# Transposes of attention probabilities in single PSUM banks instead of a pair of banks

## The chip, the cores and the metric

The kernel runs on one core of one Trainium2 chip. The metric is the time of one execution in device microseconds (us), smaller is better; the figure for the kernel before is the median of 3 runs.

## What is computed

One step of a small hybrid diffusion backbone with two trunk layers, all in float32, over 512 latent tokens and 128 context tokens with 1024 channels. Each layer projects the normed input, runs four token mixers on it, merges them through gates, and then runs a squared-ReLU MLP. Three mixers are attention: windowed grouped-query attention (8 heads), neighbourhood attention (4 heads) and multi-head latent attention (MLA, 4 heads). Cut to the part that matters here:

```python
def context_and_latent_layer(x, c, cache, lw):
    h = modulate(rms_norm(x, lw['g_attn']), sh1, sc1)
    cb, cc, cv, gq, gk, gv, nq, nk, nv, mq, mkv, mkr, gates = in_project(h, lw['w_in'])
    ...
    p = softmax_sink(jnp.concatenate([s_loc, s_ctx], axis=-1), sink)
    o = jnp.einsum('nbkgqs,nbskd->nbqkgd', p_loc, vb) + jnp.einsum('nbkgqs,nskd->nbqkgd', p_ctx, v_ctx)
    ...
    x = x + gt1 * merge_branches(gates, y_conv, y_gqa, y_na, y_mla, lw)
    x = x + gt2 * squared_relu_mlp(modulate(rms_norm(x, lw['g_mlp']), sh2, sc2), lw['w_ff1'], lw['w_ff2'])
```

## The kernel before

Every large product is made of three matmuls on float32 operands that are split in a high and a low part (`hi*hi`, `hi*lo`, `lo*hi`); the copy to `hi` is ScalarE's, the subtraction that gives `lo` VectorE's. A layer has an attention stage (`mixers`), a merge of the branches and an MLP. In the attention stage the input projections for later heads are the filler: `attend` runs the heads' blocks of 128 queries one after the other and calls `fill` between their steps, which issues some projection matmuls (L199 to L201, eight steps of three per half of the tokens).

A head has five blocks: four of latent queries and one of context queries (`ctx`). A block goes through `block_scores` (matmuls L479/L480, or L482 to L484 for MLA, then on VectorE the row minimum, L515 with a mask or L518 without), `block_exp` (ScalarE, L524), `block_norm` (the reciprocal L528 on VectorE, the product L529 on GpSimd), `block_T` (one TensorE transpose for each 128 keys, L538, then ScalarE's copy to the high part, L542), `block_lo` (VectorE's low part, L545), and, for each pair of blocks, `pair_pv` (L555, then ScalarE's copy L559) and `pair_out` (VectorE's additions into `y`, L568 to L578). The scores run three blocks ahead of the transposes: round i issues the transposes of block i, filler, the scores of block i+3, and filler.

PSUM has eight banks of 512 float32 per partition. In the attention stage they are dealt as `psum(4, 2)`: four single banks (`bank()`, tiles named `pr`: projections, `pair_pv`, MLA's products) and two pairs of banks (`banks2()`, tiles named `S2`, shown as `S` in the profile). Before the change a pair of banks serves the scores of a block, the transposes of a block and three transposes of values per layer (L414). A new tile takes a place whose earlier holder has been read for the last time; which place was chosen by the scheduler when the program was built, and TensorE waits at the new tile's first matmul until that last reader is done. TensorE's instructions stand in the order of the code. In the attention stage the order on VectorE, ScalarE, GpSimd and SyncE is the scheduler's.

A latent block has 4 or 5 pieces of 128 keys (6 in MLA), a context block has 1. Over both layers there are 160 blocks.

Of the kernel before, what the change touches and what calls it, by code (L numbers as in the profile page):

```python
# [12 lines left out]
ALU = mybir.AluOpType  # L13
# [4 lines left out]
P = 128  # L18
# [43 lines left out]
def _r(ap):  # L62
    return ap.bitcast(F32)


class Net:
# [464 lines left out]
    def block_T(self, B):  # L531
        nc = self.nc
        if B["u"] == 0:
            B["pair"]["pt"] = self.at.tile([P, 2, 6, 256], F32R, name="pt", tag="pt", bufs=2)
        pt, p, nb = B["pair"]["pt"], B["p"], B["nb"]
        tp = self.banks2()
        for i, s in enumerate(B["pos"]):
            nc.tensor.transpose(tp[:, s * P:(s + 1) * P], p[:, i * P:(i + 1) * P], self.ident)  # L538
        src = tp[:, :nb * P].rearrange("p (c q) -> p c q", q=P)
        qs = slice(B["u"] * P, (B["u"] + 1) * P)  # L540
        B["hi"], B["lo"], B["src"] = pt[:, 0, 0:nb, qs], pt[:, 1, 0:nb, qs], src
        nc.scalar.copy(B["hi"], src)  # L542

    def block_lo(self, B):
        self.nc.vector.tensor_tensor(B["lo"], B["src"], _r(B["hi"]), ALU.subtract)  # L545

    def pair_pv(self, R):

# [984 lines left out]
```

## Time and profile before

| | |
|---|---|
| median of 3 runs | 2441.95 us (2441.12 to 2443.48) |
| profiled execution, its own time | 2444.15 us |
| its span in the trace | 2442.4 us |
| TensorE busy | 2329.5 us (95%) |
| VectorE busy | 1400.2 us (57%) |
| ScalarE busy | 936.0 us (38%) |
| attention stages | about 70 to 421 us and 1265 to 1616 us of the span |

The span runs from the first to the last instruction that the profiler recorded; the execution's own time is 1.75 us longer. Busy time of TensorE is that of its matmuls, whose ends are modelled; weight loads have a row of their own (PEld). An idle time that is put down to another engine ("waited for") ends with that engine's instruction.

### The profile page before, as it was taken

Reading aid. Unit: us, or ns where it says so; the run is one execution under the profiler, and the core shown is the slowest. Engines: PE = TensorE matmul, PEld = TensorE weight load, DVE = VectorE, ACT = ScalarE, POOL = GpSimd, SP = SyncE. Lnnn points to the kernel's source line nnn. Section 1 sums busy time; section 2 is a strip of 40 time slices with the busy share of each in tenths; the row PEclk is TensorE's granted clock in tenths of the full one; section 3 lists DMA queues with packets and bytes.
Section 4 is the critical chain, followed back from the end, with each engine's and each line's share of the span. In section 5 each row is a group of like instructions: output and inputs, shape, how many; then the busy total and the mean of one; then the engine's idle time right before and its main releaser. Section 6 shows DMA issues by size and latency. Waiting matters only on the chain. (4 is left out here: it accounts for less than half of the span.)

```text
span 2442.4 us, 39683 instructions
## 1 busy us (share of the span) xinstructions
PE 2329.5 (95%) x15766; PEld 2265.1 (93%) x15766; DVE 1400.2 (57%) x2744; ACT 936.0 (38%) x1877; POOL 360.6 (15%) x468
## 2 busy tenths in 40 slices
PE   8889988999999999999998898899999999999998
PEld 4888878999999999999988897889999999999998
DVE  5776676566655777776467666753333454443433
ACT  5555554322224432322255555542222353231311
POOL 0323322111112000000123223211111110000001
PEclk9999989999999999999999999999999999999999
DMA  6322310544432344443231231033222212222222
GB/s 231 90 72 82 93 34 25 201 156 153 141 115 78 115 153 156 156 144 133 96 123 46 83 102 56 19 104 122 70 78 80 98 44 78 75 73 78 70 83 73
DMA packets 85322, 242.96 MB, mean 99 GB/s; under 512 B 9745, under 2 KB 31249, under 8 KB 83729
## 3 DMA queue, kind: packets, MB, share of 16 engines
q1 hardware_dynamic: 85136, 240.43, 29.3%
q8 instruction: 124, 2.03, 0.3%
q14 instruction: 62, 0.50, 0.1%
HBM read 222.14 MB, written 12.75 MB: 96 GB/s over the span
## 5 line engine op out<-in xcount | busy, mean ns | idle before, releaser
L199 PE MATMUL pr<-hhi,whiw 128*128 128x320 f32 (+1 forms) x2752 | 869.7, 316 | 2.7 <-ACT st L300 1.5
L201 PE MATMUL pr<-hhi,wlow 128*128 128x320 f32 (+1 forms) x2752 | 855.5, 311 | 2.3 <-DVE wlow L166 1.4
L200 PE MATMUL pr<-hlo,whiw 128*128 128x320 f32 (+1 forms) x2752 | 856.1, 311 | 0.0
L199 PEld LDWEIGHTS pr<-hhi,whiw 128*128 128x128 f32 (+1 forms) x2752 | 518.9, 189 | 4.6 <-ACT st L300 1.7
L201 PEld LDWEIGHTS pr<-hhi,wlow 128*128 128x128 f32 (+1 forms) x2752 | 518.3, 188 | 4.9 <-DVE wlow L166 2.6
L200 PEld LDWEIGHTS pr<-hlo,whiw 128*128 128x128 f32 (+1 forms) x2752 | 519.0, 189 | 3.4 <-DVE hlo L1159 2.5
L165 ACT CAST whiw<-raww 128x1024 fp32r<-128x1024 f32 x184 | 192.8, 1048 | 285.8 <-PE pr L200 266.7
L166 DVE TENSOR_TENSOR wlow<-raww,whiw 128x1024 fp32r<-128x1024 f32 x184 | 237.5, 1291 | 60.8 <-ACT whiw L165 60.2
L199 PE MATMUL pr<-hh,whiw 128*128 128x320 f32 x832 | 257.1, 309 | 0.0
L200 PE MATMUL pr<-hl,whiw 128*128 128x320 f32 x832 | 256.9, 309 | 0.0
L201 PE MATMUL pr<-hh,wlow 128*128 128x320 f32 x832 | 256.9, 309 | 0.0
L916 DVE SCALAR_TENSOR_TENSOR x<-pr,mod,x 128x256 f32<-128x256 f32 x320 | 107.7, 379 | 198.9 <-PE pr L201 196.8
L253 DVE SCALAR_TENSOR_TENSOR junk<-wm,cb 128x1024 bf16<-128x1024 f32 x160 | 195.6, 1222 | 40.9 <-DMA wm<-in_wm 37.8
L1114 POOL TENSOR_TENSOR sqs<-sqs,sq 128x320 f32<-128x320 f32 x48 | 47.6, 992 | 969.6 <-ACT sq L1112 941.9
L529 POOL TENSOR_SCALAR p<-p,sm 128x512 f32<-128x512 f32 (+3 forms) x160 | 118.6, 741 | 420.0 <-DVE sm L528 372.4
L524 ACT ACTIVATE p<-S,sm 128x641 f32<-128x641 f32 (+6 forms) x160 | 112.0, 700 | 151.0 <-DVE sm L515 78.8
L894 POOL TENSOR_TENSOR acc<-acc,sg 128x320 f32<-128x320 f32 x96 | 89.0, 931 | 521.2 <-DVE sg L893 521.1
L889 ACT ACTIVATE sg<-pr 128x320 f32<-128x320 f32 x128 | 55.6, 436 | 285.9 <-PE pr L201 280.8
L199 PEld LDWEIGHTS pr<-hh,whiw 128*128 128x128 f32 x832 | 156.4, 188 | 0.0
L200 PEld LDWEIGHTS pr<-hl,whiw 128*128 128x128 f32 x832 | 156.4, 188 | 0.0
L201 PEld LDWEIGHTS pr<-hh,wlow 128*128 128x128 f32 x832 | 156.4, 188 | 0.0
L893 DVE SCALAR_TENSOR_TENSOR sg<-sg,pr 128x320 f32<-128x320 f32 x96 | 46.1, 487 | 189.1 <-PE pr L201 189.1
(207 smaller groups left out, 3780.1 us busy)
## 6 DMA issues: line engine op xcount, KB each, us to landing
raww<-in_w SPq DMA_DIRECT2D x128, 512.0 KB, 3.5
wm<-in_wm SPq DMA_DIRECT2D x80, 512.0 KB, 3.5
raww<-in_wg SPq DMA_DIRECT2D x64, 512.0 KB, 3.8
raww<-in_wa SPq DMA_DIRECT2D x42, 512.0 KB, 3.6
wm<-in_wm SPq DMA_DIRECT2D x8, 1024.0 KB, 14.5
raww<-in_wo SPq DMA_DIRECT2D x16, 512.0 KB, 3.4
rawb<-in_wb SPq DMA_DIRECT2D x48, 128.0 KB, 2.1
kt<-kt SPq DMA_DIRECT2D x24, 224.0 KB, 3.2
```

The costliest lines, as they stand in the source:

```text
L165: nc.scalar.copy(hi, raw)
L166: nc.vector.tensor_tensor(lo, raw, _r(hi), ALU.subtract)
L199: nc.tensor.matmul(out, lhsT=whi[:, kw, :], rhs=xhi[:, kx, sl], start=(i == 0), stop=False)
L200: nc.tensor.matmul(out, lhsT=whi[:, kw, :], rhs=xlo[:, kx, sl], start=False, stop=False)
L201: nc.tensor.matmul(out, lhsT=wlo[:, kw, :], rhs=xhi[:, kx, sl], start=False, stop=(i == n - 1))
L253: nc.vector.scalar_tensor_tensor(self.junk, raw, 1.0, self.cb[v], ALU.mult, ALU.mult, accum_out=self.mod[l]["mod"][:, v, i:i + 1])
L524: nc.scalar.activation(p[:, :B["n"]], B["sc"], AF.Exp, bias=sm[:, 0:1], scale=-1.0, accum_out=sm[:, 1:2])
L529: nc.gpsimd.tensor_scalar(p[:, :n], p[:, :n], sm[:, 1:2], 1.0, ALU.mult, ALU.mult)
L889: nc.scalar.activation(sg, gp[hf][:, :HALF], AF.Tanh, scale=0.5)
L894: nc.gpsimd.tensor_tensor(a, a, sg, ALU.add)
L916: self.nc.vector.scalar_tensor_tensor(x[:, j, o + a:o + b], ps[:, a:b], m[:, v, g0 + j:g0 + j + 1], x[:, j, o + a:o + b], ALU.mult, ALU.add)
L1114: eng.tensor_tensor(self.acc[h], self.acc[h], sq, ALU.add)
```

## The change

The transposes of a block no longer take a pair of banks. Pieces 0 to 3 go to one single bank and pieces 4 and 5, where there are any, to a second one; both come from the four that the projections use. Each of the two groups has its own ScalarE copy and its own VectorE subtraction. The pairs of banks stay two, for the scores and the three value transposes.

```diff
-        tp = self.banks2()
-        for i, s in enumerate(B["pos"]):
-            nc.tensor.transpose(tp[:, s * P:(s + 1) * P], p[:, i * P:(i + 1) * P], self.ident)
-        src = tp[:, :nb * P].rearrange("p (c q) -> p c q", q=P)
         qs = slice(B["u"] * P, (B["u"] + 1) * P)
-        B["hi"], B["lo"], B["src"] = pt[:, 0, 0:nb, qs], pt[:, 1, 0:nb, qs], src
-        nc.scalar.copy(B["hi"], src)
+        B["split"] = []
+
+        for c0 in range(0, nb, 4):
+            c1 = min(nb, c0 + 4)
+            tp = self.bank()
+            for i, s in enumerate(B["pos"]):
+                if c0 <= s < c1:
+                    nc.tensor.transpose(tp[:, (s - c0) * P:(s - c0 + 1) * P], p[:, i * P:(i + 1) * P], self.ident)
+            src = tp[:, :(c1 - c0) * P].rearrange("p (c q) -> p c q", q=P)
+            B["split"].append((pt[:, 0, c0:c1, qs], pt[:, 1, c0:c1, qs], src))
+            nc.scalar.copy(B["split"][-1][0], src)
 
     def block_lo(self, B):
-        self.nc.vector.tensor_tensor(B["lo"], B["src"], _r(B["hi"]), ALU.subtract)
+        for hi, lo, src in B["split"]:
+            self.nc.vector.tensor_tensor(lo, src, _r(hi), ALU.subtract)
```

The order of TensorE's instructions, first place: early in layer 0's attention stage, from the transposes of the second block to the scores of the first head's context block. Names carry the buffer's number. Before:

```order
L538 MATMUL S2_843<-ident_92,p_743 128x128 x5
L199 MATMUL pr_813<-hhi_87,whiw_711 128x320
L200 MATMUL pr_813<-hlo_88,whiw_711 128x320
L201 MATMUL pr_813<-hhi_87,wlow_712 128x320
L199 MATMUL pr_813<-hhi_87,whiw_711 128x320
L200 MATMUL pr_813<-hlo_88,whiw_711 128x320
L201 MATMUL pr_813<-hhi_87,wlow_712 128x320
L479 MATMUL S2_856<-kt_598,qt_615 128x128
L480 MATMUL S2_856<-kt_599,qt_615 128x128
```

And in the changed kernel, at the same place:

```order
L544 MATMUL pr_843<-ident_92,p_743 128x128 x4
L544 MATMUL pr_849<-ident_92,p_743 128x128
L199 MATMUL pr_813<-hhi_87,whiw_711 128x320
L200 MATMUL pr_813<-hlo_88,whiw_711 128x320
L201 MATMUL pr_813<-hhi_87,wlow_712 128x320
L199 MATMUL pr_813<-hhi_87,whiw_711 128x320
L200 MATMUL pr_813<-hlo_88,whiw_711 128x320
L201 MATMUL pr_813<-hhi_87,wlow_712 128x320
L479 MATMUL S2_858<-kt_598,qt_615 128x128
L480 MATMUL S2_858<-kt_599,qt_615 128x128
```

No instruction of TensorE changed its place, here or elsewhere; the five transposes write two tiles. In the built programs the scores `S2_856` take the banks of the scores of the block before (`S2_820`), and start 18 matmuls after the last of those; the same scores, now `S2_858`, take those of the scores two blocks back (`S2_765`), and start 50 matmuls after them. Over both layers the median of this distance goes from 23 to 49 for scores and from 21 to 25 for transposes; for `pair_pv` it goes from 57 to 21.

Second place, TensorE later in the same stage, from `pair_pv` of a context block to the next block's transposes. Before:

```order
L555 MATMUL pr_1992<-pt_1878,vt_686 128x128 x2
L479 MATMUL S2_1999<-kt_604,qt_1064 128x128
L480 MATMUL S2_1999<-kt_605,qt_1064 128x128
L199 MATMUL pr_1961<-hhi_87,whiw_1787 128x320
L200 MATMUL pr_1961<-hlo_88,whiw_1787 128x320
L201 MATMUL pr_1961<-hhi_87,wlow_1788 128x320
L199 MATMUL pr_1961<-hhi_87,whiw_1787 128x320
L200 MATMUL pr_1961<-hlo_88,whiw_1787 128x320
L201 MATMUL pr_1961<-hhi_87,wlow_1788 128x320
L538 MATMUL S2_2017<-ident_92,p_1911 128x128 x5
```

In the changed kernel:

```order
L561 MATMUL pr_2024<-pt_1908,vt_686 128x128 x2
L479 MATMUL S2_2031<-kt_604,qt_1070 128x128
L480 MATMUL S2_2031<-kt_605,qt_1070 128x128
L199 MATMUL pr_1991<-hhi_87,whiw_1816 128x320
L200 MATMUL pr_1991<-hlo_88,whiw_1816 128x320
L201 MATMUL pr_1991<-hhi_87,wlow_1817 128x320
L199 MATMUL pr_1991<-hhi_87,whiw_1816 128x320
L200 MATMUL pr_1991<-hlo_88,whiw_1816 128x320
L201 MATMUL pr_1991<-hhi_87,wlow_1817 128x320
L544 MATMUL pr_2050<-ident_92,p_1941 128x128 x4
L544 MATMUL pr_2056<-ident_92,p_1941 128x128
```

In the built programs `S2_2017` takes the banks of the context block's scores just above it (`S2_1999`), whose last reader is the exponential; `pr_2050` takes the bank of the block before's transposes (`pr_2009`), and `pr_2056` that of the `pair_pv` just above it (`pr_2024`), whose last reader is the addition into `y`.

VectorE at that second place (`kt` are splits of keys, the last reads of the banks named above among them). Before:

```order
L214 TENSOR_TENSOR kt_1968<-st_1785,kt_1967 64x896
L518 TENSOR_REDUCE sm_2003<-S2_1999 128x1
L545 TENSOR_TENSOR pt_1918<-S2_1979,pt_1918 128x5x128
L214 TENSOR_TENSOR kt_1974<-st_1785,kt_1973 64x896
L568 TENSOR_TENSOR y_1579<-pr_1992,plo_1995 64x64 x2
L528 RECIPROCAL sm_2003<-sm_2003 128x1
L545 TENSOR_TENSOR pt_2016<-S2_2017,pt_2016 128x5x128
```

In the changed kernel:

```order
L214 TENSOR_TENSOR kt_1998<-st_1814,kt_1997 64x896
L518 TENSOR_REDUCE sm_2035<-S2_2031 128x1
L551 TENSOR_TENSOR pt_1948<-pr_2009,pt_1948 128x4x128
L214 TENSOR_TENSOR kt_2004<-st_1814,kt_2003 64x896
L574 TENSOR_TENSOR y_1602<-pr_2024,plo_2027 64x64 x2
L551 TENSOR_TENSOR pt_1948<-pr_2015,pt_1948 128x128
L528 RECIPROCAL sm_2035<-sm_2035 128x1
L551 TENSOR_TENSOR pt_2049<-pr_2050,pt_2049 128x4x128
L551 TENSOR_TENSOR pt_2049<-pr_2056,pt_2049 128x128
```

The subtraction of five pieces became two, and the second stands behind the key split and the addition into `y`.

## Rows read from the trace of the kernel before

**Rows 1.** The page: span, and busy time of each engine.

```profile
span 2442.4 us, 39683 instructions
PE 2329.5 (95%) x15766; PEld 2265.1 (93%) x15766; DVE 1400.2 (57%) x2744; ACT 936.0 (38%) x1877; POOL 360.6 (15%) x468
```

**Rows 2.** Busy time by stretch: both attention stages, then a short stretch of one.

```profile
core 0: us, PE busy (x) PEld busy (x) DVE busy (x) ACT busy (x) POOL busy (x), PEclk, DMA share, GB/s
70.00:421.00 351.00, 309.04 (x2101) 292.24 (x2099) 241.80 (x550) 194.62 (x453) 103.51 (x154) 0.94 0.20 61
1265.00:1616.00 351.00, 308.96 (x2112) 292.10 (x2111) 242.97 (x552) 195.65 (x456) 103.22 (x154) 0.94 0.20 62
...
92.20:98.40 6.20, 6.20 (x25) 6.16 (x26) 3.59 (x8) 2.87 (x7) 1.06 (x2) 0.50 0.17 65
```

**Rows 3.** Waits of TensorE's matmuls on tiles S: total us, times, longest.

```profile
PE S L479 <- ACT p L524: 22.2, 20, 2.6
PE S L482 <- ACT p L524: 18.6, 10, 2.8
...
PE S L479 <- DVE pt L545: 8.9, 10, 2.9
PE S L538 <- DVE pt L545: 7.5, 10, 1.1
...
PE S L538 <- ACT p L524: 4.4, 2, 2.2
...
PE S L414 <- ACT p L524: 2.7, 4, 1.1
...
PE S L482 <- DVE pt L545: 1.5, 2, 0.7
```

**Rows 4.** Timeline around 92 us, the first place: start, duration, instruction, [idle before].

```profile
89.19 0.31 PE L201 MATMUL pr<-hhi,wlow 128*128 128x320 f32 x1
...
91.68 0.81 DVE L545 TENSOR_TENSOR pt<-S,pt 128x640 fp32r<-128x640 f32 x1
91.89 0.19 ACT L524 ACTIVATION_READ_ACCUMULATOR p<-S,sm 128x1 f32 x1
...
92.14 0.47 PE L479 MATMUL S<-kt,qt 128*128 128x128 f32 x1 [2.64 <-ACT p L524]
```

**Rows 5.** Timeline around 193 us, the second place.

```profile
190.76 0.31 PE L201 MATMUL pr<-hhi,wlow 128*128 128x320 f32 x1
...
192.16 0.80 DVE L545 TENSOR_TENSOR pt<-S,pt 128x640 fp32r<-128x640 f32 x1
...
192.99 1.09 DVE L214 TENSOR_TENSOR kt<-st,kt 64x896 fp32r<-64x896 f32 x1
...
193.25 0.74 PE L538 MATMUL S<-ident,p 128*128 128x128 f32 x5 [2.18 <-ACT p L524]
...
194.11 0.35 DVE L568 TENSOR_TENSOR y<-pr,plo 64x64 f32<-64x64 f32 x2
```

**Rows 6.** Groups by line and form, whole run: count, busy us, mean ns, idle before.

```profile
L545 DVE TENSOR_TENSOR pt<-S,pt 128x640 fp32r<-128x640 f32 x48 | 39.4, 820 | 16.0 <-ACT pt L542 15.7
L545 DVE TENSOR_TENSOR pt<-S,pt 128x512 fp32r<-128x512 f32 x48 | 33.1, 690 | 12.0 <-ACT pt L542 11.4
L542 ACT CAST pt<-S 128x640 fp32r<-128x640 f32 x48 | 33.1, 690 | 8.5 <-PE S L538 8.2
L545 DVE TENSOR_TENSOR pt<-S,pt 128x768 fp32r<-128x768 f32 x32 | 30.6, 955 | 14.7 <-ACT pt L542 14.6
L542 ACT CAST pt<-S 128x512 fp32r<-128x512 f32 x48 | 28.0, 583 | 9.5 <-PE S L538 8.9
L542 ACT CAST pt<-S 128x768 fp32r<-128x768 f32 x32 | 25.5, 797 | 9.8 <-PE S L538 9.7
...
L545 DVE TENSOR_TENSOR pt<-S,pt 128x128 fp32r<-128x128 f32 x32 | 9.1, 285 | 0.9 <-ACT pt L542 0.5
...
L542 ACT CAST pt<-S 128x128 fp32r<-128x128 f32 x32 | 8.4, 262 | 17.9 <-PE S L538 17.8
```

## The prediction

> **What bounds the kernel now.** I read the page first: TensorE is busy for 2329.5 of 2442.4 us, no other engine for more than 57% [rows 1]. So time can only come from TensorE's gaps, or from the speed of its clock. The view of busy time by stretch says where these are: in each of the two attention stages TensorE is busy for 309 of 351 us, which leaves 42 us of gaps in each, 84 of the 113 in the whole span, and the granted clock has a mean of 0.94 there [rows 2]. The view of TensorE's waits says what ends the gaps. Seven of its rows are waits of scores, block transposes or value transposes for ScalarE's exponential (L524) or VectorE's low part (L545) [rows 3]. Neither makes an operand of these instructions. Both are the last readers of a pair of banks, so these are waits for a place: 22.2 + 18.6 + 8.9 + 7.5 + 4.4 + 2.7 + 1.5 = 65.8 us in 58 waits, 11.9 us of them at the transposes (7.5 + 4.4) and 53.9 at scores and value transposes. That is what the change can reach.
>
> The timeline shows one. TensorE's last matmul starts at 89.19 and ends at 89.50; the next scores have their operands but wait for 2.64 us, because the exponential of the block before, which held these banks, is done at 92.08 (91.89 + 0.19) [rows 4]. [...]
>
> **What the change does, step by step.**
>
> *Scores.* Two pairs of banks, taken in turn by scores and transposes, now serve scores alone but for six value transposes. The distance to the last use of the place goes from a median of 23 matmuls to 49. TensorE runs 2,101 matmuls in 309 us, 0.147 us each [rows 2], or about 0.14 where the clock is full, so the place has some 7 us to come free where it had 3.3. In the stall shown the distance grows from 18 to 50 matmuls, by 4.5 us, and the stall is 2.64: covered. I take the 53.9 us as gone at these places.
>
> *What is late next.* TensorE, no longer held at the scores, comes sooner to what follows, above all the transposes, which now share four single banks with everything else. At the first place it would start the scores at 89.50 and, 11 matmuls of 0.14 later, at 91.0, stand before the next transposes, whose first bank is held by the block before until VectorE's low part at 91.68 is done, 0.69 later with four pieces instead of 0.81 with five: 92.4 [rows 4, 6]. A stall of 2.64 turns into one of 1.3 or so. At the second place it gets worse. There the transposes wait until 193.25, 2.18 us, for an exponential. The second group of pieces now waits for the addition into `y`, which on VectorE stands behind a key split of 1.09 us and is done at 194.46 [rows 5]. TensorE would be there at 191.07 + 0.45 for the first four transposes, about 191.5, so it stalls for 2.9, 0.7 us longer than before, and scores, filler and the next `pair_pv` queue behind it.
>
> So I need a rate for the four single banks. Before, 160 blocks' transposes waited 11.9 us for a place, 0.074 us each [rows 3], at a median distance of 21 matmuls. After, 470 tiles go through the single banks: 240 of transposes (160, and 80 second groups), 96 of `pair_pv`, 134 of projections and MLA products; their distances (25 and 21 for the two I quote) are about those of the old transposes. At the same rate they wait 470 x 0.074 = 35 us. None of `pair_pv`'s and the projections' tiles waited for a place before. The bounds: nothing, if VectorE and ScalarE use the room to catch up; or all of the 65.8 us, if they only lag by as much somewhere else. I take 35, about in the middle, since of the two worked places one gains and one loses. Saved: 65.8 - 35 = 31 us.
>
> *Clock.* A mean of 0.94 over the 309 us that TensorE is busy in a stage is a loss of 0.06 x 309 = 18.5 us, 37 for both [rows 2]. Bank waits are 65.8 of 84 us of gaps (78%), and of these I let 31 of 65.8 go (47%): 37 x 0.78 x 0.47 = 13.6 us. But the ones that I worked out to remain are the long ones, such as the one that the slow stretch followed; I take half, 7 us (bounds 0 and 29, which is 78% of 37).
>
> *Added work.* 80 blocks have two groups: 48 of five pieces, 32 of six. On VectorE five pieces cost 0.820 in one instruction and 0.690 + 0.285 in two, 0.155 more; on ScalarE 0.690 against 0.583 + 0.262, again 0.155 [rows 6]. Six pieces were 0.955 and 0.797. Two pieces alone have no row; from one piece (0.285, 0.262) to four (0.690, 0.583) each piece adds 0.135 and 0.107, which gives 0.420 and 0.369, so again about 0.155 on each engine. In all 80 x 0.155 = 12.4 us on each. Beside it lies TensorE's own work while these engines are idle, 31% of the attention stages for VectorE (242 of 351 busy) and 45% for ScalarE [rows 2]. Without that cover both would sit in the release of a bank, 24.8 us. A bank was waited for at 58 of 320 places (160 scores, 160 transposes), 18% [rows 3], so I charge 18% of 24.8, 4.5 us. [...]
>
> TensorE itself does the same transposes in the same order, so it costs nothing there. Copies can start after four transposes instead of five or six, about 0.1 to 0.2 us sooner for the first group; I leave that to the bounds.
>
> **Sum.** 31 + 7 - 4.5 = 33.5 us saved. The span goes from 2442.4 to 2408.9, that execution from 2444.15 to 2410.6; the median of the runs is 2.2 us below it, so I forecast 2408.5, rounded to 2409 us.
>
> **Rivals.**
>
> *All of it goes.* The score waits vanish and VectorE, idle for 31% of the stage, keeps up, so that no wait for a place remains: 65.8 + 29 us of clock, 2442 - 95 = 2347. For it speaks that the waits are small (58, mean 1.1 us); against it the second place, where the bank is late by the trace's own times.
>
> *The stalls only move.* PSUM has the same eight banks, and what holds them is the lag of VectorE and ScalarE, which nothing shortens. `pair_pv` loses most of its distance. Then the four single banks wait for about what the pairs did, and the time is 2442 within some 5 us.
>
> *Slower.* The added instructions decide: VectorE runs in order, and where it works without a pause, as it does in the burst at 193 us [rows 5], each added 0.155 us, and each read put behind a key split, is passed on to TensorE. If all of VectorE's 12.4 us arrive and the stalls otherwise only move, it is 2442 + 12 = 2454. It decides once the waits at single banks exceed 65.8 us, twice my rate per tile. [...] VectorE's idle share speaks against it, the second place for it.
>
> **How the numbers follow.** A run of this kernel can tell about 0.2%, 5 us, from no change. I give my forecast, a saving of 12 to 55 us (2387 to 2430, from rates one and a half times and half of mine), 0.57; all of it goes (below 2387), 0.16; the stalls only move 0.15, of which two thirds lie within 5 us and the rest is a little faster; slower 0.12. So faster 0.78, same 0.10, slower 0.12. The range of 8 in 10 goes from 2366, in the middle of the way to the first rival, to 2446.
>
> **What would show it.** Waits of scores for L524 and for the low part should nearly vanish. New waits should stand at transposes (L544), at `pair_pv` (L561) and at projections and MLA products (L199 and others), ended by the low part, by ScalarE's copy of `pair_pv` and by the additions into `y`, and come to about 35 us. TensorE's gaps in each attention stage should fall from 42 to about 27 us, the granted clock rise to about 0.95, and both stages become some 17 us shorter; merge and MLP should not change. The subtractions and copies should show 240 instructions each instead of 160, with 12 us more in all. I am wrong if the new waits come to 60 us or more, or if VectorE's lag at the low part grows so that `pair_pv`'s operands are late.

## The result, and the profile after

The changed kernel takes 2405.16 us (median of 4 runs, 2403.09 to 2406.07) against 2441.53 us for the kernel before (median of 4, 2439.74 to 2443.48): a ratio of 0.985, 95% interval 0.9833 to 0.9867. The forecast was 2409.

The page of the changed kernel, span and busy time of each engine:

```profile
span 2404.3 us, 39859 instructions
PE 2314.4 (96%) x15766; PEld 2253.5 (94%) x15766; DVE 1406.3 (58%) x2824; ACT 939.8 (39%) x1957; POOL 365.6 (15%) x468
```

The span is 38.1 us shorter than in [rows 1]. TensorE's gaps (span less its busy time) go from 2442.4 - 2329.5 = 112.9 to 2404.3 - 2314.4 = 89.9 us, which is 23.0 of the 38.1. The other 15.1 us are busy time, for the same 15,766 matmuls: they ran at a higher granted clock, 0.986 on the mean of the span where it was 0.981. The medians differ by 36.4 us, so a part of this, up to 2 us, can be the spread of the runs. VectorE's busy time grew by 6.1 us and ScalarE's by 3.8.

Busy time by stretch in the changed kernel: both attention stages, and the merge and MLP between them.

```profile
70.00:404.50 334.50, 301.68 (x2095) 286.65 (x2096) 243.83 (x587) 195.37 (x493) 105.97 (x154) 0.95 0.21 64
1246.00:1579.00 333.00, 302.56 (x2114) 286.66 (x2113) 244.76 (x592) 197.62 (x497) 105.69 (x154) 0.96 0.21 65
...
404.50:1246.00 841.50, 837.15 (x5695) 832.12 (x5694) 547.68 (x966) 267.20 (x473) 77.99 (x78) 1.00 0.40 138
```

And the merge and MLP between the stages in the kernel before:

```profile
421.00:1265.00 844.00, 837.63 (x5697) 832.36 (x5696) 547.21 (x966) 267.43 (x473) 77.91 (x78) 1.00 0.40 137
```

Against [rows 2] the two stages are 16.5 and 18.0 us shorter, their gaps are 32.8 and 30.4 us instead of 42, and the mean granted clock is 0.95 and 0.96 instead of 0.94. The stretch between them has gaps of 4.4 us, where it had 6.4, and a granted clock of 1.00 as before. So 34.5 of the 38.1 us were gained in the attention stages.

TensorE's waits in the changed kernel (total us, times, longest):

```profile
PE pr L544 <- DVE pt L551: 14.0, 14, 3.3
...
PE pr L544 <- DVE S L508: 5.7, 2, 2.8
...
PE pr L561 <- DVE vt L214: 3.1, 2, 1.6
PE S L483 <- DVE qt L214: 3.1, 2, 1.7
...
PE pr L199 <- DVE y L574: 2.5, 2, 1.2
PE pr L561 <- ACT st L300: 2.2, 2, 1.1
...
PE pr L1389 <- DVE kt L214: 1.9, 2, 1.0
PE S L482 <- ACT qt L213: 1.8, 2, 0.9
PE pr L544 <- DVE y L574: 1.7, 2, 0.9
PE pr L561 <- DVE y L584: 1.6, 2, 0.8
...
PE pr L199 <- DVE pt L551: 1.4, 2, 0.7
PE pr L1389 <- ACT pt L547: 1.3, 1, 1.3
PE pr L544 <- DVE vt L214: 1.3, 2, 0.7
...
PE pr L544 <- DVE kt L214: 1.2, 2, 0.6
...
PE pr L1368 <- DVE pt L551: 1.0, 2, 0.5
PE pr L561 <- DVE pt L551: 0.9, 2, 0.5
...
PE S L479 <- ACT p L524: 0.6, 2, 0.3
```

Of the 65.8 us in [rows 3] one row of 0.6 us is left at tiles S. At the single banks, the built program gives the bank that each waiting tile takes, and its last reader. By it, waits for a place are: at the transposes (L544) 14.0 + 5.7 + 1.7 + 1.3 + 1.2 = 23.9 us, at `pair_pv` (L561) 3.1 + 2.2 + 1.6 + 0.9 = 7.8, at projections (L199) 2.5 + 1.4 = 3.9, and at MLA's products (L1389, L1368) 1.9 + 1.3 + 1.0 = 4.2. Together that is 39.8 us; rows that end with an operand and smaller rows are not assigned. Two rows are new waits of MLA's scores for their queries, 3.1 + 1.8 = 4.9: TensorE now comes there before VectorE and ScalarE have split them. So 65.8 - 0.6 - 39.8 = 25.4 us of waits went and 4.9 came, 20.5 net, most of the 23.0 of the gaps.

The row that names L508 has to be looked at, since L508 writes a column of scores that a transpose doesn't read. The timeline of the changed kernel around 106 us (start, duration, instruction, [idle before]):

```profile
104.63 0.80 POOL L529 TENSOR_SCALAR p<-p,sm 128x640 f32<-128x640 f32 x1 [1.44 <-DVE sm L528]
...
104.98 1.11 DVE L380 TENSOR_TENSOR qt<-st,qt 64x640 fp32r<-64x640 f32 x1 [0.45 <-ACT qt L379]
...
106.12 0.42 DVE L584 TENSOR_TENSOR y<-pr,plo 64x256 f32<-64x256 f32 x1
106.47 0.14 DVE L508 COPY S<-nsink 128x1 f32<-128x1 f32 x1
...
106.69 1.24 PE L544 MATMUL pr<-ident,p 128*128 128x128 f32 x5 [2.85 <-DVE S L508]
```

The transposes' bank is that of a `pair_pv`, and its last reader is the addition into `y` (L584), which ends at 106.54. It stands behind a query split of 1.11 us. L508 ends only 0.07 us later and is named for that. The probabilities had been ready since 105.43.

### The profile page after: what moved, and what is told of

It is laid out like the page before. It is cut to its first block, busy times and chain, and to the rows that moved or that the text cites. A ratio compares the mean times of both kernels' runs of the same rounds, so it can differ in the third digit from the quotient of the medians.

```text
span 2404.3 us, 39859 instructions
## 1 busy us (share of the span) xinstructions
PE 2314.4 (96%) x15766; PEld 2253.5 (94%) x15766; DVE 1406.3 (58%) x2824; ACT 939.8 (39%) x1957; POOL 365.6 (15%) x468
## 5 line engine op out<-in xcount | busy, mean ns | idle before, releaser
L199 PE MATMUL pr<-hhi,whiw 128*128 128x320 f32 (+1 forms) x2752 | 869.3, 316 | 6.8 <-DVE y L574 2.5
L199 PEld LDWEIGHTS pr<-hhi,whiw 128*128 128x128 f32 (+1 forms) x2752 | 518.5, 188 | 10.6 <-issue 3.3
L199 PE MATMUL pr<-hh,whiw 128*128 128x320 f32 x832 | 257.1, 309 | 0.0
L529 POOL TENSOR_SCALAR p<-p,sm 128x512 f32<-128x512 f32 (+3 forms) x160 | 123.8, 774 | 383.0 <-DVE sm L528 311.0
L524 ACT ACTIVATE p<-S,sm 128x641 f32<-128x641 f32 (+6 forms) x160 | 112.0, 700 | 147.2 <-DVE sm L515 78.8
L199 PEld LDWEIGHTS pr<-hh,whiw 128*128 128x128 f32 x832 | 156.4, 188 | 0.0
```

What stands on the lines that cost most here:

```text
L199: nc.tensor.matmul(out, lhsT=whi[:, kw, :], rhs=xhi[:, kx, sl], start=(i == 0), stop=False)
L524: nc.scalar.activation(p[:, :B["n"]], B["sc"], AF.Exp, bias=sm[:, 0:1], scale=-1.0, accum_out=sm[:, 1:2])
L529: nc.gpsimd.tensor_scalar(p[:, :n], p[:, :n], sm[:, 1:2], 1.0, ALU.mult, ALU.mult)
```

## Experiments

Each kernel was compared with the kernel before on the same chip. Gaps are again the span less TensorE's busy time, both from the page.

### e2_one_score_pair: the change, with one pair of banks fewer

```diff
-            self.ps_stack.enter_context(self.psum(4, 2))
+            self.ps_stack.enter_context(self.psum(4, 1))
```

> The changed kernel with one pair of banks for scores instead of two, two banks unused. Theory: scores again wait for the exponential of the block before, some 54 us of waits, on top of most of the 43 us at single banks; 2450 us (2435 to 2465). Rival (the release of transposes by single banks is what counts, the scores' second pair is not): 2405 us, within 8.

It took 2454.10 us, 1.0047 (1.0032 to 1.0062): the whole gain is gone. TensorE's waits:

```profile
PE S L479 <- ACT p L524: 32.7, 26, 3.7
PE S L482 <- ACT p L524: 21.5, 14, 2.3
```

These two rows are back, at 54.2 us. The scores' second pair is needed, even when nothing but scores and six value transposes uses it. The theory's other term did not come: it had most of 43 us at single banks on top, and the rows there come to some 13. It seems that TensorE, held at the scores, comes to these banks later.

### e3_three_singles: the change, with one single bank fewer

```diff
-            self.ps_stack.enter_context(self.psum(4, 2))
+            self.ps_stack.enter_context(self.psum(3, 2))
```

> The changed kernel with three single banks instead of four, one bank unused. Theory (the lag of VectorE and ScalarE moved to the single banks, which are now the scarce ones): the distance to the last use falls by a quarter and the waits at single banks rise from 43 us to 80 to 110; 2450 us (2435 to 2480). Rival (what is left of the waits comes from VectorE's pace, not from the number of places): not over 2412 us.

It took 2470.97 us, 1.0117 (1.0102 to 1.0132). TensorE's waits:

```profile
PE pr L561 <- DVE pt L551: 20.2, 14, 2.2
...
PE pr L199 <- DVE pt L551: 13.0, 8, 4.8
```

The scores don't wait for an exponential any more, but the tiles at single banks wait. (`pt` is an operand of L561 too, but by the built program these tiles take the bank that the subtraction frees.) Gaps are 2467.8 - 2329.6 = 138.2 us. So with four single banks the change sits near the edge: with one less it would have ended on the slower side.

### e5_six_singles_one_pair: all eight banks, but only one pair

```diff
-            self.ps_stack.enter_context(self.psum(4, 2))
+            self.ps_stack.enter_context(self.psum(6, 1))
```

> The changed kernel with six single banks and one pair for scores. Theory (scores need a second pair; single banks are the place that is short after the change): the waits at single banks nearly vanish, the scores' waits are the 54 us of the kernel with one pair and four singles, which lacks only the two added singles; 2435 us (2425 to 2450). Rival (the waits at single banks are VectorE's pace and follow TensorE wherever it goes): as with one pair and four singles, 2454 us, within 5.

It took 2444.55 us, 1.0009 (0.9999 to 1.002): no gain. That lies inside the theory's range, 10 us above its point. TensorE's waits:

```profile
PE S L479 <- ACT p L524: 34.7, 28, 3.7
PE S L482 <- ACT p L524: 27.6, 18, 3.3
```

With six single banks the waits there for the low part are small (the largest row is 2.0 us, L561 for L551). But 62.3 us of score waits take up what this gives.

### e1_split_in_pairs and e6_split_after_all: the split alone, transposes kept in a pair

The first attempt only changed where the two groups lie:

```diff
+        pair = self.banks2()
         for c0 in range(0, nb, 4):
             c1 = min(nb, c0 + 4)
-            tp = self.bank()
+            tp = pair[:, c0 * P:]
```

> The split alone: copy and subtraction in groups of four pieces and the rest, but the transposes stay in a pair of banks. Theory (the gain comes from the scores no longer taking turns with transposes for two pairs of banks): the score waits stay at about 54 us, the two extra instructions cost about 4.5 us, 2446 us (2440 to 2452). Rival (the gain comes from the smaller groups, whose copies start sooner, or from the other order that they bring on VectorE and ScalarE): about 2405 us.

It took 2511.26 us, 1.0281 (1.0266 to 1.0296), far more than either theory gave. TensorE's waits say why:

```profile
PE S L545 <- ACT pt L548: 85.0, 80, 2.7
```

All 80 second groups waited for the copy of the first group. They write the other bank of the pair, but it is the same tile, and the program orders them behind its reader. The edit had added a wait of its own, so this run says nothing on the split. In the next one all transposes stand ahead of both copies:

```diff
+        pair = self.banks2()
+        for i, s in enumerate(B["pos"]):
+            nc.tensor.transpose(pair[:, s * P:(s + 1) * P], p[:, i * P:(i + 1) * P], self.ident)
         for c0 in range(0, nb, 4):
             c1 = min(nb, c0 + 4)
-            tp = self.bank()
-            for i, s in enumerate(B["pos"]):
-                ...
+            tp = pair[:, c0 * P:]
```

> The split alone once more, without the wait that the first try had added: all transposes of a block go to the pair of banks first, then come the two copies and later the two subtractions. Theory (the gain is in the places, the split only costs): score waits near 54 us as before, 4 us for the added instructions, 2446 us (2440 to 2454). Rival (smaller groups or the other order on VectorE and ScalarE bring the gain): about 2405 us.

It took 2449.72 us, 1.0032 (1.0023 to 1.0042): the split alone costs some 8 us (0.0032 x 2442.6), and gives nothing. TensorE's waits:

```profile
PE S L540 <- DVE pt L551: 22.7, 19, 3.3
```

The waits are of the same kind as in [rows 3]; transposes waited 7.5 us for the low part there, and 22.7 us here. The scores' largest row stays, at 20.7 us for L524.

### e4_groups_of_two: the change, with twice the copies and subtractions

```diff
-            B["split"].append((pt[:, 0, c0:c1, qs], pt[:, 1, c0:c1, qs], src))
-            nc.scalar.copy(B["split"][-1][0], src)
+            for a in range(c0, c1, 2):
+                b = min(c1, a + 2)
+                B["split"].append((pt[:, 0, a:b, qs], pt[:, 1, a:b, qs], src[:, a - c0:b - c0]))
+                nc.scalar.copy(B["split"][-1][0], src[:, a - c0:b - c0])
```

> The changed kernel with each group of four pieces copied and subtracted in two instructions of two pieces: 128 more on each engine. By the changed kernel's rows this adds 128 x (2 x 0.414 - 0.687) = 18 us on VectorE and 128 x (2 x 0.380 - 0.583) = 23 us on ScalarE. Theory (18% of the added work reaches TensorE): 7 us, 2412 us (2405 to 2418). Rival (VectorE sets the pace, each added us arrives): 18 us or more, 2423 us and up.

It took 2409.51 us, 0.9867 (0.9851 to 0.9884), 4.35 us more than the change, with intervals that overlap. The page:

```profile
PE 2317.2 (96%) x15766; PEld 2256.1 (94%) x15766; DVE 1410.7 (59%) x2952; ACT 948.8 (39%) x2085; POOL 365.7 (15%) x468
```

Both engines run 128 instructions more. By mean durations these add the 18 and 23 us named above. But records of neighbouring instructions overlap (the last section shows two on VectorE that take 0.88 us where their means give 0.970), and the busy times grew by only 1410.7 - 1406.3 = 4.4 us on VectorE and 948.8 - 939.8 = 9.0 on ScalarE. TensorE's gaps are 2407.4 - 2317.2 = 90.2 us, as after the change (89.9). So the rival's 18 us don't arrive, and VectorE's added work opens no gaps. The few us by which the time is longer are no clear difference.

### e8_three_pairs: the kernel before, with three pairs and two single banks

```diff
-            self.ps_stack.enter_context(self.psum(4, 2))
+            self.ps_stack.enter_context(self.psum(2, 3))
```

> The kernel before with three pairs of banks and two single banks, nothing split. Theory (a wait for a place depends on how far back its last use lies): waits at the pairs fall from 66 us to about 20, but 230 tiles now share two singles at half the distance, at about the rate of the old transposes, 17 us or more; 2425 us (2410 to 2450). Rival (giving scores and transposes places of their own is what helps, more places in common do not): 2442 us or more.

Nothing is split here and transposes still take a pair. It took 2404.05 us, 0.9845 (0.983 to 0.9859), as fast as the change, and 21 us below what I had expected. TensorE's busy time and waits:

```profile
PE 2313.6 (96%) x15766; PEld 2250.9 (94%) x15766; DVE 1402.1 (58%) x2744; ACT 935.1 (39%) x1877; POOL 367.1 (15%) x468
```

```profile
PE pr L199 <- ACT st L300: 8.7, 9, 1.8
...
PE pr L199 <- DVE y L578: 5.9, 5, 1.8
...
PE pr L199 <- DVE y L568: 2.5, 2, 1.2
```

The waits at the pairs nearly go: for L524 and the low part, 0.4 + 2.2 us are left at scores and 2.4 + 2.0 at transposes, 7.0 in all, where I had expected about 20 (a row of 4.3 us more at the transposes names no releaser). The two single banks are the next stop, as expected: their 230 tiles wait for a place, the projections for 17.1 us in these three rows (1.5 of it stands in the kernel before too), and MLA's products (L1362) for 2.3 + 1.8 + 1.6 = 5.7. Gaps are 2403.5 - 2313.6 = 89.9 us, the same as after the change. What the expectation had left out is the clock: TensorE is busy for 15.9 us less than before, at a mean granted clock of 0.988 instead of 0.981.

### e7_pv_freed_early, e9_three_pairs_pv_freed, e10_before_pv_freed: `pair_pv`'s bank freed by ScalarE

ScalarE copies both halves of `pair_pv`, so that its bank comes free without VectorE, and the addition into `y` moves from VectorE to GpSimd. The same edit was made in the change (e7), in the kernel with three pairs (e9) and in the kernel before (e10):

```diff
         nc.scalar.copy(R["plo"][:, :n], ps[64:P, :n])
+        nc.scalar.copy(R["phi"][:, :n], ps[0:64, :n])
...
-        ps, lo, pr = R["ps"], R["plo"], R["pr"]
+        ps, lo, pr = R["phi"], R["plo"], R["pr"]
...
-            nc.vector.tensor_tensor(y[rows, pr * HALF:pr * HALF + HL], ps[0:64, :256], lo, ALU.add)
+            nc.gpsimd.tensor_tensor(y[rows, pr * HALF:pr * HALF + HL], ps[:, :256], lo, ALU.add)
```

> The changed kernel with the single bank of the value product freed by ScalarE: it copies both halves (0.37 us more for a pair of blocks), and the addition into y moves from VectorE to GpSimd, from SBUF. Theory (what is left are late releases of single banks, about 11 us of them by these additions): these waits go, some clock comes back, and VectorE loses some 30 us of work; 2392 us (2380 to 2404). Rival (ScalarE's 96 added copies, some 32 us, stand ahead of its copies of transposes and exponentials and make these late): 2405 us or more.

In the change it took 2396.53 us, 0.9815 (0.9801 to 0.983), the fastest kernel here, 8.6 us below the change itself. Its page and TensorE's waits:

```profile
PE 2318.3 (97%) x15766; PEld 2257.4 (94%) x15766; DVE 1371.5 (57%) x2680; ACT 968.1 (40%) x2053; POOL 445.5 (19%) x612
```

```profile
PE pr L544 <- issue: 8.7, 6, 2.1
...
PE pr L544 <- DVE pt L551: 6.2, 8, 1.9
```

Gaps are 2397.5 - 2318.3 = 79.2 us. The row that ended with L508 is gone, and the 14.0 us for the low part are 6.2. But a row of 8.7 us is new, for which the profile names no releaser (`issue`), and all rows of the transposes (L544) come to 26.5 us, where they were 27.6. The timeline of e7 at the second place of the prediction:

```profile
184.96 0.26 ACT L567 COPY phi<-pr 64x128 f32<-64x128 f32 x1
...
185.32 0.74 PE L544 MATMUL pr<-ident,p 128*128 128x128 f32 x5 [2.07 <-issue]
```

The transposes start 0.10 us after ScalarE's new copy has ended: the bank of `pair_pv` is freed by ScalarE now, and it is still waited for. What fell are waits elsewhere, by all their rows: at `pair_pv` from 8.0 to 4.9 us, at projections from 6.5 to 3.2, at MLA's products (L1389 and L1368 in the change) from 4.2 to 1.9, and those of MLA's scores for their queries from 4.9 to 0.8. VectorE, which splits queries and reads banks at many of these places, is busy for 34.8 us less. So e7 gains, but whether by the earlier release or by VectorE's shorter queue is not shown.

> Three pairs and two single banks, nothing split, with the value product's bank freed by ScalarE and the addition into y on GpSimd. Theory (the two steps remove waits at different places, so they add): of the waits at single banks some 8 us end with the addition into y and go, some clock comes back; 2392 us (2382 to 2399). Rival (with two singles the projections' own lag decides, and ScalarE's added copies lengthen it): 2402 us or more.

With three pairs it took 2401.40 us, 0.9835 (0.9821 to 0.9848), which can't be told from e8. The theory missed: the wait of the projections moves from the addition to ScalarE's own copy (`PE pr L199 <- ACT phi L561` holds 8.1 us in 10 waits).

> The kernel before, with only the value product's bank freed by ScalarE and the addition into y on GpSimd. Theory (the gain of that step is the freed bank; here no single bank is waited for, and the waits are at the pairs): at most a little from VectorE's lighter work, 2440 us (2434 to 2448). Rival (that step gains by taking 30 us off VectorE): as much as on the changed kernel, 2433 us or less.

In the kernel before it took 2452.07 us, 1.0042 (1.0028 to 1.0055), slower, where the theory had no change or a little less, and the rival a gain from VectorE's relief (1369.8 us busy, 30 less than before). TensorE's waits:

```profile
PE S L538 <- DVE pt L545: 11.1, 11, 2.1
PE S L482 <- ACT p L524: 10.2, 8, 2.7
...
PE S L538 <- ACT p L524: 7.0, 4, 2.5
```

The rows at the transposes grew, from 7.5 and 4.4 us [rows 3], but the row of MLA's scores (L482) fell, from 18.6, and the seven rows of [rows 3] come to 66.6 us, 0.8 more than before. Gaps are 2449.4 - 2335.4 = 114.0 us, 1.1 more. The rest of the longer span is TensorE's busy time, 5.9 us more, at a mean granted clock of 0.978 instead of 0.981; why, is open. So 30 us less on VectorE bring nothing while the pairs are what is waited for. That doesn't settle what they bring in e7, where the pairs are not.

## Why the prediction was right

**Scores: right, and shown.** 53.9 us of waits at scores and value transposes were to go; 0.6 are left. That the cause is the number of places that scores find free, and not the split, is shown from three sides: the split without single banks (e6) loses 8 us, the single banks without the second pair (e2, e5) give nothing back, and a third pair without any split (e8) gives as much as the change.

**What is late next: the total nearly right by luck, its shares not.** I took 0.074 us for each of 470 tiles, 35 us. The rows sum to 39.8. But the 240 tiles of transposes wait 23.9 us, 0.100 each, and the 230 others 15.9, 0.069 each. The rate was no property of a tile: in e8, the same 230 tiles at two single banks wait for 22.8 us in the rows named there alone, where the rate gives 17, and scores and transposes at three pairs for 7.0 in the rows that name L524 or the low part, where I had 20.

**The two worked places: the first right, the second right in size and half in cause.** The timeline of the changed kernel at the first place:

```profile
89.39 0.88 DVE L551 TENSOR_TENSOR pt<-pr,pt 128x512 fp32r<-128x512 f32 x2
...
90.22 0.73 PE L544 MATMUL pr<-ident,p 128*128 128x128 f32 x5 [0.88 <-DVE pt L551]
```

The stall of 2.64 at the scores [rows 4] became one of 0.88 at the next transposes, for the low part; I had 1.3. At the second place:

```profile
184.21 0.63 PE L544 MATMUL pr<-ident,p 128*128 128x128 f32 x4 [1.88 <-DVE pt L551]
...
185.71 0.45 PE L544 MATMUL pr<-ident,p 128*128 128x128 f32 x1 [0.87 <-DVE y L574]
```

The stall of 2.18 [rows 5] became 1.88 + 0.87 = 2.75 us; I had 2.9. The second part, for the addition into `y`, was forecast. The first was not: I had the first four transposes start at once, and they wait for the low part of the block before. The addition is also the release of the stall at 106 us above. In e7, where ScalarE frees that bank, the second place still waits for 2.07 us.

**Added work: right by the rows, too large by the engines' time.** Groups by line and form in the changed kernel:

```profile
L551 DVE TENSOR_TENSOR pt<-pr,pt 128x512 fp32r<-128x512 f32 x128 | 87.9, 687 | 26.0 <-ACT pt L547 24.9
L547 ACT CAST pt<-pr 128x512 fp32r<-128x512 f32 x128 | 74.6, 583 | 22.2 <-PE pr L544 21.2
...
L551 DVE TENSOR_TENSOR pt<-pr,pt 128x128 fp32r<-128x128 f32 x80 | 22.7, 283 | 0.9 <-ACT pt L547 0.5
L547 ACT CAST pt<-pr 128x128 fp32r<-128x128 f32 x80 | 21.6, 270 | 17.5 <-PE pr L544 17.3
L551 DVE TENSOR_TENSOR pt<-pr,pt 128x256 fp32r<-128x256 f32 x32 | 13.3, 414 | 0.1
L547 ACT CAST pt<-pr 128x256 fp32r<-128x256 f32 x32 | 12.1, 380 | 1.1 <-PE pr L544 0.9
```

Both have 240 instructions. Their sums are 123.9 and 108.3 us, 11.7 and 13.3 more than in [rows 6], where I had 12.4 on each. But neighbouring records overlap (the two subtractions at 89.39 take 0.88 us, not the 0.970 of their means), and the engines' busy times grew by only 6.1 and 3.8 us. No run shows the 4.5 us that I charged for it: in e4, VectorE's busy time grows by another 4.4 us and the gaps don't.

**Gaps and clock: two terms mis-sized, in opposite ways.** The sum had 31 - 4.5 = 26.5 us from gaps and 7 from the clock, 33.5; measured are 23.0 and 15.1, 38.1. In the gaps, 39.8 us of waits are left at the single banks, close to my 35 and 4.5 more for the added work. I had left out that scores, once they come sooner, can be too early for their operands: 4.9 us at MLA's scores. For the clock I had worked out 13.6 and then halved it, because the stalls that I expected to remain were long ones (the slow stretch that I named there is the last line of [rows 2], which begins where the stall of [rows 4] ends). Long ones do remain (up to 3.3 us), and 15.1 us came all the same. So it was the halving that was wrong: no run shows the 7 us, nor that long stalls cost more of the clock than short ones. The gaps gave 3.5 us less than forecast and the clock 8.1 more; that the time is only 4 us from 2409 is in part luck. Which stalls cost how much clock is left open: e3 has 48 us more of gaps than the change, and a mean granted clock of 0.985 against 0.986, with 15.2 us more busy time.

**The rivals.** "All of it goes" fails, with 33 and 30 us of gaps left in the stages. "The stalls only move" fails in this kernel, but e3 shows it: one single bank less, and they move and grow. "Slower", with VectorE setting the pace, fails by the time itself, and by e4, where more added instructions than in the change open no gaps. That a lighter VectorE would speed up the changed kernel is not excluded (e7).

## What to carry to other kernels

Where a saturated engine waits for places in a buffer, list for each kind of tile how many places it shares, with whom, and how long its last reader takes; here the kind that is read late, a score, read by an exponential, had too few of them (53.9 us of waits, together with the value transposes), and it was enough to give it places of its own (0.6 us in the change) or one more in common (0.4 + 2.2 us at scores in e8). Try the plain count of places before restructuring: three pairs instead of two gave here, in one line, what the split and the single banks gave. Then look at the waits at the new place, here for the low part and for the addition into `y` behind a split. The edit that gave the latter to another engine brought 8.6 us after the change, nothing clear with three pairs, and a loss before the change; so it has to be tried in the kernel at hand.

## What the runs showed of the hardware

The clock's share was larger than expected: 15.1 of 38.1 us came as shorter busy time of the same matmuls, at a mean granted clock of 0.986 instead of 0.981. It doesn't follow the gaps alone: the kernel of e3 has 48 us more of gaps than the change, a granted clock of 0.985 and only 15.2 us more busy time, while e10 has 1.1 us more of gaps than the kernel before, a granted clock of 0.978 and 5.9 us more busy time. (e7 has 10.7 us less of gaps than the change, a granted clock of 0.984 and 3.9 us more busy time, but its profiled execution is 2.9 us above the median of its runs.)

Two neighbouring subtractions on VectorE overlap in the record: four pieces and one take 0.88 us back to back (the row at 89.39), where the groups give 0.687 + 0.283 = 0.970 for the two alone and 0.820 for all five in one [rows 6]. Splitting an instruction cost 0.06 us there, not 0.155.

The additions of 64x256 into `y` were slower on GpSimd, even from copies in SBUF: one took 0.773 us there, as the groups of e7 show, and 0.42 on VectorE (the row at 106.12). The kernel of e7 was still faster. One of TensorE's waits there, 2.0 us, names an addition on GpSimd (`PE pr L544 <- POOL y L584`).

```profile
L586 POOL TENSOR_TENSOR y<-phi,plo 64x256 f32<-64x256 f32 x48 | 37.1, 773 | 48.3 <-ACT phi L567 47.4
```
